# The norm of queries and keys in an encoder layer: eps from a 65th column, the mean's factor in the square's scale

## The chip, the cores and the metric

The kernel runs on one core of a Trainium2 chip. The metric is the device time of one execution in microseconds (us). A core has five engines with an instruction queue each, which run side by side and wait for each other through semaphores: PE (matrix products; its weight loads are listed as PEld), DVE (vector operations), ACT (activations and scaled copies), POOL (a slower general engine) and SP, which here issues the transfers (DMA). An engine takes its own instructions strictly in the order written, so one that waits holds up all behind it.

## The reference

The kernel computes one layer of a hybrid encoder for two sequences with shared weights, 512 tokens (P, "prompt") and 1024 tokens (S, "sample"), 1024 wide, in float32. Cut to what matters here:

```
h = rmsnorm(x, norm_g); proj = h @ w_in
qa, ka, va, za, qb, kb, vb, zb, ga, gb = split(proj)
qa = rmsnorm(qa.reshape(B, L, 8, 64), qn_a);  ka = rmsnorm(ka.reshape(B, L, 8, 64), kn_a)
oa = neighbourhood_attention(qa, ka, va, rpb_a) * silu(za) @ w_o_a      # branch A: 8 heads
qb = rmsnorm(qb.reshape(B, L, 8, 64), qn_b);  kb = rmsnorm(kb.reshape(B, L, 2, 64), kn_b)
ob = window_gqa_attention(qb, kb, vb, t5_table, sink_b) * silu(zb) @ w_o_b   # branch B: 8 query, 2 key heads
y = x + (sigmoid(ga) * oa + sigmoid(gb) * ob) @ w_out

rmsnorm(x, g) = x * rsqrt(mean(x * x) + 1e-6) * g      # over the 64 channels of a head
```

## The kernel before

**Precision.** Every large product is made of three: each operand is split into a rounded part and a rest (hi and lo), and hi·hi, lo·hi and hi·lo are summed in PSUM. ACT writes the rounded part (a copy with a change of type), DVE or POOL subtracts it for the rest (L1172 and L1177 in the dense part, L605 and L610 for the attention weights).

**Stages.** First P's attention, then P's dense part, then S's attention, then S's dense part; the orders overlap where data allow. Attention goes by six groups of heads: four of branch A (two query and two key heads each), two of branch B (four query heads and one key head). For each group and each tile of 128 tokens `project` makes one projection of 384 columns: 24 matmuls (L764) into a PSUM bank p. P has 6 x 4 = 24 such projections and S 6 x 8 = 48, 72 in all, 48 of branch A and 24 of branch B.

**The norm, once per projection.** From the bank p: ACT squares the 4 or 5 heads' columns into sq (L783), DVE sums 64 columns for each head (`tensor_reduce`, L788), POOL multiplies by 1/64 and adds eps (`tensor_scalar`, L795), POOL raises to the power -0.5 (L802), and DVE multiplies q and k by that factor into qk (L819; for branch B the key half by L669 on DVE or L665 on ACT). Beside it ACT and DVE take the values v out of the bank (L809, L812). Then PE transposes qk (L864), ACT and DVE write the transposed parts (L885 to L904), and the scores (L937, L972), the softmax (L981, L1005, and a scaling on POOL L1011 or DVE L1013), the transposes of its result (L1029) and the product with v (L1066) follow. The tile sq has one buffer, so a Square waits for the reduce before it.

**The order.** A planner (`Flow`) records each operation with its engine or engines, a cost in ns, a priority and what it depends on; `run` then plays the operations through a clock of its own, gives each to a free engine by priority, and writes the instructions of every engine in that order. Costs count: an operation that the planner believes to end sooner lets others stand elsewhere, on any engine. Costs of ACT, DVE and POOL in the attention are taken times 1.1 (SLACK), and a hop between engines has its own cost (LAG; 96 ns from POOL to POOL). Operations that DVE or POOL can do go to the one that the planner thinks done first.

Of the kernel before, what the change touches and what calls it, by code (L numbers as in the profile page):

```python
# [40 lines left out]
P = 128  # L41
# [3 lines left out]
EPS = 1e-6  # L45
# [309 lines left out]
def encoder_kernel(  # L355
# [23 lines left out]
    nc = tc.nc  # L379
    act = nc.scalar  # L380
    dve = nc.vector
# [35 lines left out]
    mhalf = cpool.tile([P, 8], F32, tag="mhalf", name="mhalf")  # L417
# [10 lines left out]
    DVE_ = lambda n: 68 + 1.043 * n  # L428
# [3 lines left out]
    f = Flow(pspool)  # L432

    def bank(tag):
        return f.value(pspool, [P, 512], F32, tag, BANKS[tag])
# [215 lines left out]
    def attention_phase(geo, hh, hl, h_ops, mask_d, early, late):  # L651
# [6 lines left out]
        def tile_(shape, dt, tag, bufs):  # L658
            return f.value(early if tag in ("sq", "ss", "rs_v", "rs_r", "v", "q", "qt", "qk") else late, shape, dt, tag, bufs)
# [3 lines left out]
        def copy(e, out, in_, scale=None):  # L663
# [4 lines left out]
            else:  # L668
                engines[e].tensor_scalar(out, in_, scale, None, op0=ALU.mult)  # L669

        a_tables = geo.tables()
        at = np.cumsum([0, *(n for n, _ in a_tables)]).tolist()
        mask = tile_([P, at[-1]], F32, "mask", 1)
# [57 lines left out]
        def project(br, w, t, prio):  # L731

            nq, nk = (2, 2) if br == "A" else (4, 1)
            nn = nq + nk
            ps = bank("p")
# [22 lines left out]
            for k in range(KC):  # L758
                hi, lo = w[k // 2]
                c = slice((k % 2) * GW, (k % 2) * GW + GW)  # L760
                for m, (u, mv) in enumerate(((0, hi), (0, lo), (1, hi))):
# [19 lines left out]
            f.op(  # L781
                (("act", ACT_(nn * 64, False)),),
                lambda e: act.activation(sq.t[:, : nn * 64], ps.t[:, : nn * 64], AF.Square),  # L783
                prio, new=[sq], use=[ps],
            )
            f.op(
                (("dve", DVE_(nn * 64)),),
                lambda e: dve.tensor_reduce(  # L788
                    ss.t[:, :nn], sq.t[:, : nn * 64].rearrange("p (h d) -> p h d", d=64), axis=AX.X, op=ALU.add
                ),  # L790
                prio, new=[ss], use=[sq],
            )
            f.op(
                (("pool", 165),),
                lambda e: nc.gpsimd.tensor_scalar(  # L795
                    rv.t[:, :nn], ss.t[:, :nn], 1.0 / 64, EPS, op0=ALU.mult, op1=ALU.add
                ),
                prio, new=[rv], use=[ss],
            )
            f.op(  # L800
                (("pool", 1000),),
                lambda e: nc.gpsimd.tensor_tensor(r.t[:, :nn], rv.t[:, :nn], mhalf[:, :nn], op=ALU.pow),  # L802
                prio, new=[r], use=[rv],
            )
            nv = GW - nn * 64

# [6 lines left out]
                prio, use=[ps, v], into=[v],  # L813
# [9 lines left out]
                    op=ALU.mult,  # L823
                ),
                prio, new=[qk], use=[ps, r],
# [285 lines left out]
        for gi, (br, g) in enumerate(groups):  # L1111
# [14 lines left out]
            for t in range(nb):  # L1126
                prio = lead + t
# [673 lines left out]
    for i in range(2):  # L1801
        ps, made = bank("x"), []
        for j in range(2):
# [3 lines left out]
                lambda e, ps=ps, cols=cols, out=out: pe.matmul(ps.t[:, out], one, gb.t[:1, cols], start=True, stop=True),  # L1807
# [3 lines left out]
    for t in range(gp.nb):  # L1811
# [4 lines left out]
        for i, (ps, users) in enumerate(gains_row if t == 0 else ()):  # L1816
            gains_row[i][1] = [f.op(
                (("act", ACT_(512, False)),),
                lambda e, ps=ps, i=i: act.activation(gb.t[:, i * 512 : i * 512 + 512], ps.t, AF.Copy),
                NORM[1] - 1, use=[ps], hold=[gb], after=users[2:],  # L1820
            )]
    setup(norm_p, -0.7, h_ops["p"][1][:1])
    expand_ops(gp, [max(-1, (h // 2 - 1) * gp.nb) for h in range(8)], [h_ops["p"][t][:1] for t in (1, 3, 3, 3)])
    o_p, exps, start = attention_phase(gp, *h_p, h_ops["p"], mask_p, early["p"], late["p"])
    rb = f.value(rb_pool, [P, NT_S], F32, "rb", 1)
    r_s = f.value(norm_p, [P, gs.nb], F32, "r_s", 1)
    for t in range(gs.nb):
# [10 lines left out]
        after=[o, f.begun[NT_P, 23]],  # L1838
# [111 lines left out]
```

## Time and profile before

| what | before |
|---|---|
| time, median of 3 runs | 1136.74 us (1136.4 to 1139.61) |
| the profiled execution | 1139.25 us, its span 1137.5 us |
| TensorE clock granted, mean | 0.998 |
| DVE, ACT, POOL busy | 856.8, 651.4, 339.3 us |
| idle time of POOL before the scaling L795, ended by the reduce L788 | 134.0 us in 41 waits |
| power L802, shortest and median | 1006 and 1060 ns |

The span goes from the first to the last instruction of the profiled execution. A row of a group names the line, the engine, the operation, what it writes and reads, the shape and the count; then the busy time of the group in us and the mean of one instruction in ns; then the idle time of its engine just before, and what ended it. A row of the timeline has the start in us, the duration in us, the instruction, and in brackets the idle time before it and what ended that.

### The profile page before, as it was taken

The page shows a single profiled execution, that of the slowest core. Times are in us where ns is not written, and L with a number is a line of the kernel's source. Part 1 is how long each engine was busy: PE and PEld are TensorE (multiplying, and loading weights), DVE is VectorE, ACT ScalarE, POOL GpSimd, SP SyncE. Part 2 cuts the span into 40 slices and gives each one's busy share as a digit, 9 for nine tenths or more (in the row PEclk, how much of TensorE's full clock was granted, in tenths as well). Part 3 has the DMA queues.
Part 4 walks back from the last instruction along what each step waited for, and adds up shares of the span by engine and source line. Part 5 has one row for each costly group of instructions (what it writes and reads, how often), then busy time and mean ns, then how long its engine had stood idle before and what let it go on. Part 6 is the DMA issues. An engine that isn't in the chain of part 4 may idle for free.

```text
span 1137.5 us, 18703 instructions
## 1 busy us (share of the span) xinstructions
PE 1121.8 (99%) x6079; PEld 975.1 (86%) x6079; DVE 856.8 (75%) x1988; ACT 651.4 (57%) x1499; POOL 339.3 (30%) x438
## 2 busy tenths in 40 slices
PE   8999999999999999999999999999999999999998
PEld 6999988888888889999999988988788888888877
DVE  5878797587776568787878889876988766767564
ACT  5777987644532247565769888877543435333430
POOL 3654433000011144434324343510333323123111
PEclk9999999999999999999999999999999999999999
DMA  7854543488785743121213214244888645756862
GB/s 257 273 159 138 185 115 103 107 254 257 246 286 202 249 138 91 29 61 29 82 41 93 73 38 119 50 131 138 288 261 237 206 158 191 278 197 224 262 208 93
DMA packets 139108, 186.11 MB, mean 164 GB/s; under 512 B 29897, under 2 KB 68561, under 8 KB 139010
## 3 DMA queue, kind: packets, MB, share of 16 engines
q1 hardware_dynamic: 139010, 184.91, 51.8%
q8 instruction: 48, 0.79, 0.3%
q14 instruction: 50, 0.41, 0.1%
HBM read 137.66 MB, written 51.92 MB: 167 GB/s over the span
## 4 chain that ended last, share of the span: by engine, by line
PE 90%; DMA 4%; DVE 2%; ACT 1%; issue 1%; SPq 1%; POOL 0%; ACTq 0%; DVEq 0%
PE p L764 26%; PE x L1293 8%; PE x L1295 8%; PE x L1294 8%; PE x L1066 5%; PE x L1029 5%; PE x L937 5%; PE p L1294 4%; PE p L1295 4%; PE p L1293 4%; PE d L1293 4%; PE d L1295 4%; PE d L1294 4%; PE x L864 2%; DMA w<-in_w_att_dram 1%; DMA U<-m_d 1%
## 5 line engine op out<-in xcount | busy, mean ns | idle before, releaser
L764 PE MATMUL p<-whi,hh 128*128 128x384 f32 x384 | 133.7, 348 | 0.0
L764 PE MATMUL p<-whi,hl 128*128 128x384 f32 x384 | 132.6, 345 | 0.0
L764 PE MATMUL p<-wlo,hh 128*128 128x384 f32 x384 | 132.0, 344 | 0.0
L1172 ACT ACTIVATE whi<-raw 128x512 fp32r<-128x512 f32 (+1 forms) x140 | 81.5, 600 | 73.0 <-PE x L1294 22.5
L981 ACT ACTIVATE sb<-sb,mx 128x384 f32<-128x384 f32 (+1 forms) x192 | 107.7, 565 | 16.9 <-DVE mx L972 16.6
L1294 PE MATMUL x<-T,whi 128*128 128x512 f32 x280 | 108.9, 389 | 0.0
L1293 PE MATMUL x<-T,whi 128*128 128x512 f32 x280 | 108.9, 389 | 0.0
L1295 PE MATMUL x<-T,wlo 128*128 128x512 f32 x280 | 108.9, 389 | 0.0
L764 PE MATMUL p<-whi,hb 128*128 128x384 f32 x384 | 107.6, 346 | 0.0
L1177 DVE TENSOR_TENSOR wlo<-raw,whi 128x512 fp32r<-128x512 f32 (+1 forms) x110 | 73.4, 678 | 34.5 <-ACT whi L1172 31.0
L1177 POOL TENSOR_TENSOR wlo<-raw,whi 128x512 fp32r<-128x512 f32 (+1 forms) x30 | 36.4, 1219 | 210.2 <-ACT whi L1172 210.2
L1040 DVE TENSOR_TENSOR pp<-x,pp 128x512 fp32r<-128x512 f32 (+1 forms) x136 | 82.6, 639 | 19.2 <-ACT pp L1035 18.5
L802 POOL TENSOR_TENSOR rs_r<-rs_v,mhalf 128x4 f32<-128x4 f32 (+1 forms) x72 | 80.7, 1121 | 5.7
L1293 PE MATMUL x<-hh,whi 128*128 128x512 f32 x200 | 78.4, 392 | 2.1 <-ACT fh L1440 2.1
L1035 ACT ACTIVATE pp<-x 128x512 fp32r<-128x512 f32 (+1 forms) x136 | 70.9, 561 | 15.2 <-PE x L1029 14.0
L1295 PE MATMUL x<-hh,wlo 128*128 128x512 f32 x200 | 78.5, 393 | 0.0
L1294 PE MATMUL x<-hl,whi 128*128 128x512 f32 x200 | 78.3, 392 | 0.0
L1066 PE MATMUL x<-pp,v 128*128 128x256 f32 (+1 forms) x368 | 75.8, 322 | 0.0
L764 PEld LDWEIGHTS p<-whi,hl 128*128 128x128 f32 x384 | 72.8, 190 | 1.3 <-issue 1.0
L764 PEld LDWEIGHTS p<-wlo,hh 128*128 128x128 f32 x384 | 73.0, 190 | 1.0 <-issue 0.7
L764 PEld LDWEIGHTS p<-whi,hh 128*128 128x128 f32 x384 | 73.0, 190 | 0.7 <-DVE v L812 0.3
L764 PEld LDWEIGHTS p<-whi,hb 128*128 128x128 f32 x384 | 69.1, 188 | 3.0 <-issue 1.3
(388 smaller groups left out, 2967.8 us busy)
## 6 DMA issues: line engine op xcount, KB each, us to landing
raw<-in_w_g_dram SPq DMA_DIRECT2D x84, 256.0 KB
w<-in_w_att_dram SPq DMA_DIRECT2D x46, 384.0 KB
raw<-in_w_z_dram SPq DMA_DIRECT2D x40, 256.0 KB
ot<-o_d SPq DMA_DIRECT2D x36, 256.0 KB
g_d<-C SPq DMA_DIRECT2D x34, 256.0 KB
fr<-in_w_g_dram SPq DMA_DIRECT2D x28, 256.0 KB
raw<-in_w_out_dram SPq DMA_DIRECT2D x28, 256.0 KB
out_dram<-C SPq DMA_DIRECT2D x19, 256.0 KB
```

Source lines behind the costliest of these rows:

```text
L764: pe.matmul(ps.t[:, :GW], part[u](k), mv.t[:, c], start=k == 0 and m == 0, stop=k == KC - 1 and m == 2,)
L802: lambda e: nc.gpsimd.tensor_tensor(r.t[:, :nn], rv.t[:, :nn], mhalf[:, :nn], op=ALU.pow),
L937: pe.matmul(pss[2 * pair + i].t[:, :width], q.t[rows, u, at : at + P], kv[:, tiles[0] : tiles[-1] + 1 : step], start=n == 0, stop=n == 2,)
L981: act.activation(sb.t[:, :width], sb.t[:, :width], AF.Exp, bias=mx.t[:, i : i + 1], scale=-1.0, accum_out=sm.t[:, i : i + 1],)
L1035: lambda e, pt=pt, pp=pp, nn=nn: act.activation(pp.t[:, 0, :nn], pt.t[:, :nn], AF.Copy),
L1040: lambda e, pt=pt, pp=pp, nn=nn: dve.tensor_tensor(pp.t[:, 1, :nn], pt.t[:, :nn], pp.t[:, 0, :nn].bitcast(F32), op=ALU.subtract),
L1066: pe.matmul(out(), v.t[:, vs], mv(), start=first, stop=last)
L1172: (("act", ACT_(n)),), lambda e: act.activation(hi(), src(), AF.Copy), prio,
L1177: lambda e: engines[e].tensor_tensor(lo(), src(), hi().bitcast(F32), op=ALU.subtract), prio,
L1293: pe.matmul(out, hi.t[:, cs], mh(), start=first and k == 0, stop=False, **more)
L1294: pe.matmul(out, hi.t[:, cs], ml(), start=False, stop=False, **more)
L1295: pe.matmul(out, lo.t[:, cs], mh(), start=False, stop=last and k == len(ws) - 1, **more)
```

## The change

The tile sq is made once for a whole attention phase and has 65 columns for each of five heads. A memset on POOL at the head of the phase writes eps into each 65th column. Square is given the scale 0.125, so that it writes (x/8)^2 = x^2/64, into the first 64 columns of each head; the reduce sums 65 columns, and so gives mean plus eps. The scaling on POOL (L795) and its tile rs_v are gone, and the power reads the reduce's result. Square waits for the reduce before it, as before.

```diff
@@ -668,6 +668,9 @@
+        sq = tile_([P, 336], F32, "sq", 1)
+        sqv = lambda n: sq.t[:, : n * 65].rearrange("p (h d) -> p h d", d=65)
+        sq_ops = [f.op((("pool", 100),), lambda e: nc.gpsimd.memset(sqv(5)[:, :, 64:], EPS), -0.5, new=[sq])]
         a_tables = geo.tables()
...
@@ -773,34 +776,25 @@
-            sq = tile_([P, 320], F32, "sq", 1)
             ss = tile_([P, 8], F32, "ss", 2)
-            rv = tile_([P, 8], F32, "rs_v", 2)
             r = tile_([P, 8], F32, "rs_r", 2)
             v = tile_([P, 256], F32R, "v", 7 if nt == NT_S else 6)
             f.op(
                 (("act", ACT_(nn * 64, False)),),
-                lambda e: act.activation(sq.t[:, : nn * 64], ps.t[:, : nn * 64], AF.Square),
-                prio, new=[sq], use=[ps],
-            )
-            f.op(
-                (("dve", DVE_(nn * 64)),),
-                lambda e: dve.tensor_reduce(
-                    ss.t[:, :nn], sq.t[:, : nn * 64].rearrange("p (h d) -> p h d", d=64), axis=AX.X, op=ALU.add
+                lambda e: act.activation(
+                    sqv(nn)[:, :, :64], ps.t[:, : nn * 64].rearrange("p (h d) -> p h d", d=64), AF.Square, scale=0.125
                 ),
-                prio, new=[ss], use=[sq],
-            )
-            f.op(
-                (("pool", 165),),
-                lambda e: nc.gpsimd.tensor_scalar(
-                    rv.t[:, :nn], ss.t[:, :nn], 1.0 / 64, EPS, op0=ALU.mult, op1=ALU.add
-                ),
-                prio, new=[rv], use=[ss],
-            )
+                prio, use=[ps], hold=[sq], after=sq_ops[-1:],
+            )
+            sq_ops.append(f.op(
+                (("dve", DVE_(nn * 65)),),
+                lambda e: dve.tensor_reduce(ss.t[:, :nn], sqv(nn), axis=AX.X, op=ALU.add),
+                prio, new=[ss], hold=[sq], after=f.ops[-1:],
+            ))
             f.op(
                 (("pool", 1000),),
-                lambda e: nc.gpsimd.tensor_tensor(r.t[:, :nn], rv.t[:, :nn], mhalf[:, :nn], op=ALU.pow),
-                prio, new=[r], use=[rv],
+                lambda e: nc.gpsimd.tensor_tensor(r.t[:, :nn], ss.t[:, :nn], mhalf[:, :nn], op=ALU.pow),
+                prio, new=[r], use=[ss],
             )
```

The planner now writes another order on every engine. In the changed file lines stand elsewhere: the reduce is L791 (before L788), the power L796 (L802), v L806 (L812), qk L813 (L819), qk's transposes L858 (L864), the projection's matmuls L767 (L764), the scores L966 (L972), the reciprocal L999 (L1005), sums L1160 (L1166), subtractions L1171 (L1177), the tables L701 (L698).

At the start of S's attention, POOL before (raw<-raw are sums of weights, fl the rest of a weight in the dense part, rs_r the power's result):

```order
L1166 TENSOR_TENSOR raw<-raw 128x512 x4
L1177 TENSOR_TENSOR fl<-fr,fh 128x512
L795 TENSOR_SCALAR rs_v<-ss 128x4
L802 TENSOR_TENSOR rs_r<-rs_v,mhalf 128x4
L795 TENSOR_SCALAR rs_v<-ss 128x4
L802 TENSOR_TENSOR rs_r<-rs_v,mhalf 128x4
L698 TENSOR_TENSOR bias<-mask,raw 128x16x8
```

and now:

```order
L1160 TENSOR_TENSOR raw<-raw 128x512
L673 MEMSET sq 128x5
L1160 TENSOR_TENSOR raw<-raw 128x512 x3
L1171 TENSOR_TENSOR fl<-fr,fh 128x512
L796 TENSOR_TENSOR rs_r<-ss,mhalf 128x4 x2
L701 TENSOR_TENSOR bias<-mask,raw 128x16x8
```

The second memset stands among the four sums, and the power comes straight after fl. On PE, at the same place, 24 matmuls of the second projection are followed by three product steps of three matmuls before (L1293 to L1295, into the bank d) and by two now, and then by the transposes of qk.

In P's attention, where the second projection's qk is made, DVE before (xt is a tile of x that is being normed, hl the rest of its transposed norm, bias a table):

```order
L523 SCALAR_TENSOR_TENSOR xt<-xt,nr,rb 128x512
L698 TENSOR_TENSOR bias<-mask,raw 128x32x4
L698 TENSOR_TENSOR bias<-mask,raw 128x16x4 x3
L698 TENSOR_TENSOR bias<-mask,raw 128x32x4 x2
L698 TENSOR_TENSOR bias<-mask,raw 128x16x4 x4
L523 SCALAR_TENSOR_TENSOR xt<-xt,nr,rb 128x512
L545 TENSOR_TENSOR hl<-x,hh 128x4x128
L812 TENSOR_TENSOR v<-p,v 128x2x64
L819 TENSOR_TENSOR qk<-p,rs_r 128x256
```

and now:

```order
L806 TENSOR_TENSOR v<-p,v 128x2x64
L545 TENSOR_TENSOR hl<-x,hh 128x4x128
L701 TENSOR_TENSOR bias<-mask,raw 128x32x4
L701 TENSOR_TENSOR bias<-mask,raw 128x16x4 x4
L701 TENSOR_TENSOR bias<-mask,raw 128x32x4
L701 TENSOR_TENSOR bias<-mask,raw 128x16x4 x4
L523 SCALAR_TENSOR_TENSOR xt<-xt,nr,rb 128x512 x2
L813 TENSOR_TENSOR qk<-p,rs_r 128x256
```

The second subtraction for hl and that for v no longer stand between L523 and qk.

In P's branch B, the 20th projection, DVE before, from its reduce on:

```order
L788 TENSOR_REDUCE ss<-sq 128x5
L1616 COPY fc<-d 128x512
L667 CAST hb<-hl 128x512
L1177 TENSOR_TENSOR fl<-fr,fh 128x512
L1005 RECIPROCAL rs<-sm 128x4
L972 ISA sb,mx<-x,bias,nsink 128x384
L972 ISA mx 128x1
L812 TENSOR_TENSOR v<-p,v 128x64
```

and now:

```order
L791 TENSOR_REDUCE ss<-sq 128x5
L806 TENSOR_TENSOR v<-p,v 128x64
L667 CAST hb<-hl 128x512
L1171 TENSOR_TENSOR fl<-fr,fh 128x512
L813 TENSOR_TENSOR qk<-p,rs_r 128x256
L999 RECIPROCAL rs<-sm 128x4
L669 TENSOR_SCALAR qk<-p,rs_r 128x128
```

Before, three more scores follow those rows, then qk (L819), a cast to hb and the key half (L669). So a copy and four scores stood ahead of qk, and now none does. On PE 56 instructions stood between that projection's last matmul and the transposes of its qk; now 30 do.

More of the change, by code (lines that the diff above doesn't have):

```diff
@@ L782, in project @@
                 (("act", ACT_(nn * 64, False)),),
-                lambda e: act.activation(sq.t[:, : nn * 64], ps.t[:, : nn * 64], AF.Square),
-                prio, new=[sq], use=[ps],
-            )
-            f.op(
-                (("dve", DVE_(nn * 64)),),
-                lambda e: dve.tensor_reduce(
-                    ss.t[:, :nn], sq.t[:, : nn * 64].rearrange("p (h d) -> p h d", d=64), axis=AX.X, op=ALU.add
-                ),
-                prio, new=[ss], use=[sq],
-            )
-            f.op(
-                (("pool", 165),),
-                lambda e: nc.gpsimd.tensor_scalar(
-                    rv.t[:, :nn], ss.t[:, :nn], 1.0 / 64, EPS, op0=ALU.mult, op1=ALU.add
-                ),
-                prio, new=[rv], use=[ss],
-            )
+                lambda e: act.activation(
+                    sqv(nn)[:, :, :64], ps.t[:, : nn * 64].rearrange("p (h d) -> p h d", d=64), AF.Square, scale=0.125
+                ),
+                prio, use=[ps], hold=[sq], after=sq_ops[-1:],
+            )
+            sq_ops.append(f.op(
[3 more added lines that the diff above has]
+            ))
             f.op(
                 (("pool", 1000),),
-                lambda e: nc.gpsimd.tensor_tensor(r.t[:, :nn], rv.t[:, :nn], mhalf[:, :nn], op=ALU.pow),
-                prio, new=[r], use=[rv],
+                lambda e: nc.gpsimd.tensor_tensor(r.t[:, :nn], ss.t[:, :nn], mhalf[:, :nn], op=ALU.pow),
+                prio, new=[r], use=[ss],
             )
```

## The prediction

> **What bounds the kernel now.** I read the page's busy times first, then who waited for whom on PE, then the groups of the norm's instructions, and last the timeline at each place where PE stood still. The first row of the page, and the waits of PE (waiter, released by, then us in total, times, the longest):
>
> ```profile
> PE 1121.8 (99%) x6079; PEld 975.1 (86%) x6079; DVE 856.8 (75%) x1988; ACT 651.4 (57%) x1499; POOL 339.3 (30%) x438
> ...
> PE x L1807 <- DMA rb<-in_norm_row_dram: 4.6, 1, 4.6
> PE x L864 <- DVE qk L819: 2.4, 2, 1.9
> PE x L1293 <- ACT fh L1440: 2.1, 1, 2.1
> PE d L1294 <- DVE T L1177: 1.3, 1, 1.3
> PE x L535 <- DVE xt L523: 1.0, 1, 1.0
> PE p L1293 <- ACT whi L1172: 0.5, 1, 0.5
> ```
>
> PE is the bound, and hardly ever waits: 1137.5 - 1121.8 = 15.7 us of the span are free, and these six rows are 11.9 of them. Only the second row belongs to what is changed: 2.4 us, in two places, in which the transposes of qk (L864) wait for the multiplication by the norm's factor (L819). That is 0.2% of the time. The other 70 norms are hidden: PE works on later projections, scores or dense products until qk is there. So shortening the norm can win 2.4 us at most by itself; whatever else happens comes from the planner, which orders all engines anew when one cost changes.
>
> **The change part by part.** The groups of the norm before, by shape (count, then busy us and mean ns of one, then idle before):
>
> ```profile
> L802 POOL TENSOR_TENSOR rs_r<-rs_v,mhalf 128x4 f32<-128x4 f32 x48 | 51.0, 1064 | 3.7
> L795 POOL TENSOR_SCALAR rs_v<-ss 128x4 f32<-128x4 f32 x48 | 15.3, 318 | 101.0 <-DVE ss L788 99.5
> ...
> L783 ACT ACTIVATE sq<-p 128x256 f32<-128x256 f32 x48 | 18.4, 383 | 15.2 <-PE p L764 12.3 <-DVE qk L819 1.3 <-ACT q L899 0.5
> L809 ACT ACTIVATE v<-p 128x128 fp32r<-128x128 f32 x48 | 13.3, 277 | 0.0
> L783 ACT ACTIVATE sq<-p 128x320 f32<-128x320 f32 x24 | 10.4, 435 | 1.1 <-PE p L764 1.0
> ...
> L788 DVE TENSOR_REDUCE ss<-sq 128x4 f32<-128x256 f32 x48 | 19.7, 411 | 5.1 <-ACT sq L783 4.9
> ```
>
> *Removed:* 72 scalings on POOL (L795), 318 ns each in the mean over the 48 of branch A: some 23 us of POOL's 339.3, and as much from the chain Square, reduce, scaling, power, multiplication. POOL is 30% busy, so its time as such is worth nothing; the chain is covered by PE's other work in all but the two places.
>
> *Square:* it now writes 64 columns, leaves one, and so on, and its scale is no longer one. The row of L809 writes with gaps too. From 256 to 320 columns Square grows by 435 - 383 = 52 ns, 0.81 ns a column, so 128 columns without gaps would take 279; L809 takes 277. A gap costs nothing: 0. *Reduce:* 4 or 5 columns more on 256 or 320; if all of its 411 ns went with the columns, 4 x 1.6 = 6.4 ns each, 0.5 us on DVE in 72, hidden since DVE has a quarter of the span free: 0, and at most 0.5 bare.
>
> *Two memsets added on POOL.* The timeline of POOL, with idle time before in brackets:
>
> ```profile
> 0.24 0.10 POOL L1929 MEMSET const-float32-0.0<- 128x1 f32 x1 [0.24 <-issue]
> ...
> 5.53 0.19 POOL L467 TENSOR_SCALAR nv<-ns 128x1 f32<-128x1 f32 x1 [4.24 <-ACT junk L463]
> ...
> 390.83 1.80 POOL L1166 TENSOR_TENSOR raw<-raw 128x512 f32<-128x512 f32 x1 [13.29 <-DVE raw L1166]
> ```
>
> A small memset is 0.10 us. The first stands ahead of 4.24 us in which POOL idles, the second among the four sums of L1166, before the last of which POOL idles 13.29 us. Both 0; bare, 0.10 each. Behind them are queued the identity's second half and the next sum, which have that same idle time.
>
> *The place at 406 us,* where the second sequence's attention starts. POOL, DVE, PE:
>
> ```profile
> 404.49 1.31 POOL L1177 TENSOR_TENSOR fl<-fr,fh 128x512 fp32r<-128x512 f32 x1 [11.86 <-ACT fh L1172]
> 405.88 1.17 POOL L795 TENSOR_SCALAR rs_v<-ss 128x4 f32<-128x4 f32 x1
> 407.13 1.01 POOL L802 TENSOR_TENSOR rs_r<-rs_v,mhalf 128x4 f32<-128x4 f32 x1
> 408.23 0.19 POOL L795 TENSOR_SCALAR rs_v<-ss 128x4 f32<-128x4 f32 x1
> ...
> 404.89 2.10 DVE L667 CAST hb<-hl 128x512 fp32r<-128x512 f32 x2
> 408.18 0.42 DVE L819 TENSOR_TENSOR qk<-p,rs_r 128x256 f32<-128x256 f32 x1 [0.69 <-POOL rs_r L802]
> ...
> 405.18 0.39 PE L1293 MATMUL d<-hh,fh 128*128 128x512 f32 x1
> 405.87 0.39 PE L1293 MATMUL d<-hh,fh 128*128 128x512 f32 x1
> 408.66 0.44 PE L864 MATMUL x<-ident,qk 128*128 128x128 f32 x2 [1.94 <-DVE qk L819]
> ```
>
> Here the scaling took 1.17 us where the next one took 0.19, and ended as DVE's two casts did (404.89 + 2.10 = 406.99). With it gone the power starts at 405.88. Either it is held by the casts as the scaling was, ends at about 407.05 + 1.01 = 408.06 instead of 408.14, and saves 0.08; or it runs at once, ends at 406.89, and qk follows the casts at 407.0, 1.18 earlier. The nearest row is the scaling itself, an instruction of the same engine at the same moment: 0.08. Against that, the planner counts on the shorter chain: PE's order has two product steps of three matmuls ahead of L864 where it had three, one step of 405.87 - 405.18 = 0.69 us put behind it. PE arrives 0.69 earlier and waits for the same chain: 0.69 - 0.08 = **+0.6 us**, with bounds 0.69 - 1.18 = -0.5 and +0.6. The Trainium skill, "SBUF — State Buffer", § Who interferes with whom, has a rule that speaks against this part of the change: a cast on VectorE in its two-port mode takes the port pair that it shares with GpSimd for a whole instruction, and the other engine blocks until the end. The 1.17 beside 0.19 agrees; by that rule it would be the +0.6, without it the -0.5.
>
> *The place at 30 us.* DVE, and PE behind it:
>
> ```profile
> 28.60 0.82 DVE L523 SCALAR_TENSOR_TENSOR xt<-xt,nr,rb 128x512 f32<-128x512 f32 x1
> 29.34 0.68 DVE L545 TENSOR_TENSOR hl<-x,hh 128x512 fp32r<-128x512 f32 x1
> 29.94 0.27 DVE L812 TENSOR_TENSOR v<-p,v 128x128 fp32r<-128x128 f32 x1
> 30.14 0.41 DVE L819 TENSOR_TENSOR qk<-p,rs_r 128x256 f32<-128x256 f32 x1
> ...
> 30.69 0.41 PE L864 MATMUL x<-ident,qk 128*128 128x128 f32 x2 [0.48 <-DVE qk L819]
> ```
>
> The factor was long there; qk stood behind L545 and L812 on DVE. In the new order both are out of its way (one later, one earlier), so it can start up to 30.14 - 29.34 = 0.8 us sooner, and the wait of 0.48 goes: **-0.5**, bounds -0.5 and 0.
>
> *Everything the planner moves beside that.* PE's rows at the end of the part that is reordered and behind it:
>
> ```profile
> 813.95 0.50 PE L1294 MATMUL d<-T,whi 128*128 128x512 f32 x1 [1.30 <-DVE T L1177]
> ...
> 821.22 0.39 PE L1293 MATMUL x<-T,whi 128*128 128x512 f32 x1
> ...
> 1085.98 0.50 PE L1293 MATMUL x<-hh,whi 128*128 128x512 f32 x1 [2.09 <-ACT fh L1440]
> ```
>
> PE has the same instructions, and its last 1375 of 6076, from the row at 821.22 on, stand in the same order, with the wait of 2.1 for L1440 among them; so do the 831 that end just before the place at 406 us, with the wait of 0.5 for L1172. Neither goes. The wait of 1.3 for T lies where the order is new: gone or doubled, -1.3 to +1.3; I take 0, since nothing in the change touches T or its subtraction.
>
> Sum: 0.6 - 0.5 = **+0.1 us** on the profiled execution's 1139.25 (span 1137.5 and 1.75 around it), and the same on the median of the runs, 1136.74, which is 2.5 below it: **1136.8**. From the bounds alone: -0.5 - 0.5 - 1.3 = -2.3, and 0.6 + 0.2 + 0.5 + 1.3 = +2.6.
>
> **The rivals.** (1) *Faster:* the time that POOL and the chain gain empties the waits. All of those that lie where the order is new would go: 2.4 and 1.3, so 1136.7 - 3.7 = **1133.0**. For it: PE waits nowhere else. Against it: half of this is the place at 406 us, where the casts hold POOL whatever it runs. Beyond this there is nothing to win, since PE's own work is the same.
>
> (2) *Slower:* the new order moves L864 forward on PE further than the chain gets shorter. Its place is branch B, where DVE has the longest queues. At 147 us:
>
> ```profile
> 147.42 0.47 DVE L788 TENSOR_REDUCE ss<-sq 128x5 f32<-128x320 f32 x1
> 152.45 0.41 DVE L819 TENSOR_TENSOR qk<-p,rs_r 128x256 f32<-128x256 f32 x1
> 153.33 0.34 DVE L669 TENSOR_SCALAR qk<-p,rs_r 128x128 f32<-128x128 f32 x1
> ...
> 152.75 0.34 PE L764 MATMUL p<-wlo,hb 128*128 128x384 f32 x1
> 152.92 1.04 PE L1029 MATMUL x<-ident,sb 128*128 128x128 f32 x8
> 153.71 0.59 PE L764 MATMUL p<-whi,hb 128*128 128x384 f32 x2
> 154.32 0.49 PE L864 MATMUL x<-ident,qk 128*128 128x128 f32 x3
> ```
>
> Between the projection's last matmul and L864 PE has 56 instructions before and 30 now; 14 of L764 (152.92 - 152.75 = 0.17 apart), the eight of L1029 (0.79 until the next) and one product step of 0.69 are gone, 3.9 us of cover. There was 154.32 - 153.67 = 0.65 to spare. If qk and its key half came as late after the reduce as before, less the scaling's 0.32, PE would stand 3.9 - 0.65 - 0.3 = 2.9 us. The order says otherwise: four scores, a copy and an idle moment are no longer ahead of qk on DVE, nor a cast ahead of the key half. But that is the planner's reckoning, and other places in branch B lose cover too (78 instructions to 32 at one in the second sequence). It decides from a little over one such place; two make 1136.8 + 5.8 = **1142.6**.
>
> (3) *The change doesn't do what it says:* a gap in Square's output, or a power that takes over the scaling's waits, leaves the chain as long as it was. Then only the +0.69 and the -0.5 remain: 1136.9, inside the forecast.
>
> **How the numbers follow.** A measurement of this kernel tells about 0.3%, 3.4 us, from no change. The forecast with (3) has 0.66, (1) 0.13, (2) 0.21. (1) just reaches 0.3%, so faster by more is 0.12, and the rest of it goes to no change; (2) is slower. No change: 0.67. The bounds of the terms give 1134.5 to 1139.3 for the likeliest case alone; to leave out no more than 2 in 10, I go down to (1) and up most of the way to (2): 1133.0 to 1141.5.
>
> **What would show it.** Right: PE busy within 1 us of 1121.8; no L795; Square and reduce within 10 ns of their rows; the wait of L864 at the start of the second sequence's attention at 1.9 to 2.7 us and that at 30 us gone; POOL's power there ending with or after DVE's casts. Wrong: waits of PE for L819 or L669 in branch B that add up to over 3 us, or a sum of PE's waits under 9 us.

## The result, and the profile after

| | before | after |
|---|---|---|
| time, median of 6 runs | 1138.17 us (1136.40 to 1139.92) | 1146.82 us (1142.51 to 1150.65) |
| the profiled execution, its span | 1139.25, 1137.5 us | 1145.95, 1144.2 us |
| sum of PE's idle time, PE busy | 15.7, 1121.8 us | 20.6, 1123.6 us |

The ratio of the runs is 1.0071 with a 95% interval of [1.0045, 1.0097]. The change makes the kernel 0.7% slower. The forecast was no change, 1136.8 us in a range of 1133.0 to 1141.5; the kernel is slower than all of that range.

The first row of after's page, the busy times:

```profile
PE 1123.6 (98%) x6079; PEld 975.1 (85%) x6079; DVE 857.9 (75%) x1971; ACT 652.1 (57%) x1502; POOL 322.7 (28%) x382
```

And the waits of PE (waiter, released by, then us in total, times, the longest):

```profile
PE x L1801 <- DMA rb<-in_norm_row_dram: 4.6, 1, 4.6
PE x L858 <- DVE qk L813: 3.3, 5, 1.4
PE x L1287 <- ACT hh L1166: 3.1, 1, 3.1
PE x L1060 <- DVE pp L1034: 1.4, 1, 1.4
PE x L535 <- DVE xt L523: 1.1, 1, 1.1
PE x L1023 <- DVE sb L1007: 1.1, 2, 0.9
PE d L1287 <- ACT fc L1610: 1.1, 2, 0.7
PE x L1287 <- ACT fh L1434: 1.0, 1, 1.0
```

The third of these rows is new, and it is the longest single wait that before doesn't have. Nothing in it belongs to the norm: PE waits for hh, the rounded part of a gated row in P's dense part. PE's timeline there:

```profile
358.28 0.40 PE L1289 MATMUL x<-hh,wlo 128*128 128x512 f32 x1
361.79 0.50 PE L1287 MATMUL x<-hh,whi 128*128 128x512 f32 x1 [3.12 <-ACT hh L1166]
...
363.54 0.63 PE L1288 MATMUL x<-hl,whi 128*128 128x512 f32 x1
363.96 0.63 PE L1289 MATMUL x<-hh,wlo 128*128 128x512 f32 x1
...
367.20 0.39 PE L1289 MATMUL x<-hh,wlo 128*128 128x512 f32 x1
367.43 0.40 PE L1287 MATMUL x<-hh,whi 128*128 128x512 f32 x1
```

Two things are to be seen. PE stands still for 3.12 us. And for some 3.5 us after it the same matmul starts every 0.42 to 0.43 us and lasts 0.63; by 367 us it is back to 0.23 and 0.39. The busy time by stretch has that as a granted clock (the number after the busy times, ahead of the share of the DMA engines) under 1:

```profile
340.00:350.00 10.00, 10.00 (x46) 8.28 (x45) 7.33 (x12) 4.92 (x9) 1.30 (x1) 1.00 0.75 234
...
360.00:365.00 5.00, 2.98 (x8) 2.19 (x9) 3.02 (x5) 1.26 (x2) 0.00 (x0) 0.81 0.77 251
365.00:370.00 5.00, 5.00 (x21) 4.03 (x20) 1.94 (x3) 1.90 (x3) 0.00 (x0) 0.85 0.64 175
370.00:380.00 10.00, 10.00 (x46) 8.29 (x45) 4.17 (x7) 0.79 (x2) 1.28 (x1) 1.00 0.88 293
```

5 x (1 - 0.81) + 5 x (1 - 0.85) = 1.7 us are lost behind the wait. Matched matmul by matmul, PE in after is 2.0 us later than before from 219 to 357 us, and 7.8 at 378. So 5.8 of the 6.7 us by which the two profiled executions differ arise here, in a stretch in which PE's order did not change. The rest nearly cancels: +2.0 in P's attention, -1.1 between this place and S's attention, +2.7 in S's attention, and -2.7 at 1086 us, where the profile of before has its wait of 2.09 us with a lower clock behind it.

Why hh was late is read from ACT and PE. Before, hh was written at 354.24 + 0.63 = 354.87, and PE read it at 356.26 without a wait, 1.39 us later:

```profile
354.24 0.63 ACT L1172 ACTIVATE hh<-C 128x512 fp32r<-128x512 f32 x1 [4.57 <-DVE C L1166]
...
356.26 0.39 PE L1293 MATMUL x<-hh,whi 128*128 128x512 f32 x1
```

After, the same row of ACT stands 6.87 us later, while PE would have come 2.0 later:

```profile
361.11 0.63 ACT L1166 ACTIVATE hh<-C 128x512 fp32r<-128x512 f32 x1 [4.54 <-DVE C L1160]
```

6.87 - 2.02 - 1.39 = 3.46, which is the delay to 0.05 us (of which 3.12 is idle time). The lateness builds up in a chain beside PE (load of x, norm, store, gate, hh): in P's dense part DVE also norms S's x, two tiles at a time, from x loaded by SP (L558) into two buffers, and DVE and SP take the gates, the weights' rests (wlo) and those loads in turn. SP's last pair of x loads starts at 297.61 us in the timeline of before:

```profile
297.61 1.78 SPq L558 DMA_DIRECT2D xt<-in_xt_s_dram  x2
```

and at 302.58 in that of after:

```profile
302.58 1.84 SPq L558 DMA_DIRECT2D xt<-in_xt_s_dram  x2
```

That is 5.0 us late, of which PE's own lateness explains 2.0. In this stretch the order of SP, DVE and ACT did change, although PE's did not.

### The profile page after: what moved, and what is told of

It reads as the page before. It is cut to its first block, busy times and chain, and to the rows that moved or that the text cites. A ratio compares the mean times of both kernels' runs of the same rounds, so it can differ in the third digit from the quotient of the medians.

```text
span 1144.2 us, 18686 instructions
## 1 busy us (share of the span) xinstructions
PE 1123.6 (98%) x6079; PEld 975.1 (85%) x6079; DVE 857.9 (75%) x1971; ACT 652.1 (57%) x1502; POOL 322.7 (28%) x382
## 4 chain that ended last, share of the span: by engine, by line
PE 75%; DMA 9%; DVE 6%; issue 4%; ACT 3%; POOL 2%; SPq 1%; POOLq 0%; ACTq 0%; DVEq 0%
PE p L767 21%; PE x L1287 6%; PE x L1288 6%; PE x L1289 6%; PE x L1060 5%; PE x L1023 4%; PE x L931 4%; PE d L1287 3%; PE d L1289 3%; PE d L1288 3%; PE p L1287 3%; PE p L1289 3%; PE p L1288 3%; DMA w<-in_w_att_dram 2%; PE x L858 2%
## 5 line engine op out<-in xcount | busy, mean ns | idle before, releaser
L767 PE MATMUL p<-whi,hh 128*128 128x384 f32 x384 | 133.7, 349 | 0.0
L767 PE MATMUL p<-wlo,hh 128*128 128x384 f32 x384 | 131.9, 344 | 0.0
L767 PE MATMUL p<-whi,hl 128*128 128x384 f32 x384 | 131.9, 344 | 0.1
L796 POOL TENSOR_TENSOR rs_r<-ss,mhalf 128x4 f32<-128x4 f32 (+1 forms) x72 | 89.4, 1242 | 140.6 <-DVE ss L791 136.1
L1166 ACT ACTIVATE whi<-raw 128x512 fp32r<-128x512 f32 (+1 forms) x140 | 81.7, 600 | 76.0 <-PE x L1288 24.4
L767 PE MATMUL p<-whi,hb 128*128 128x384 f32 x384 | 107.0, 346 | 0.0
L1171 DVE TENSOR_TENSOR wlo<-raw,whi 128x512 fp32r<-128x512 f32 (+1 forms) x111 | 74.8, 683 | 32.4 <-ACT whi L1166 26.6
L1171 POOL TENSOR_TENSOR wlo<-raw,whi 128x512 fp32r<-128x512 f32 (+1 forms) x29 | 35.3, 1223 | 211.1 <-ACT whi L1166 211.0
L767 PEld LDWEIGHTS p<-whi,hl 128*128 128x128 f32 x384 | 72.8, 190 | 1.5 <-issue 1.0
L767 PEld LDWEIGHTS p<-whi,hh 128*128 128x128 f32 x384 | 72.8, 190 | 0.7 <-issue 0.5
L767 PEld LDWEIGHTS p<-wlo,hh 128*128 128x128 f32 x384 | 72.9, 190 | 0.5 <-issue 0.5
L767 PEld LDWEIGHTS p<-whi,hb 128*128 128x128 f32 x384 | 69.4, 188 | 3.2 <-issue 0.8
```

Source lines behind the costliest of these rows:

```text
L767: pe.matmul(ps.t[:, :GW], part[u](k), mv.t[:, c], start=k == 0 and m == 0, stop=k == KC - 1 and m == 2,)
L796: lambda e: nc.gpsimd.tensor_tensor(r.t[:, :nn], ss.t[:, :nn], mhalf[:, :nn], op=ALU.pow),
L1166: (("act", ACT_(n)),), lambda e: act.activation(hi(), src(), AF.Copy), prio,
L1171: lambda e: engines[e].tensor_tensor(lo(), src(), hi().bitcast(F32), op=ALU.subtract), prio,
```

## The experiments

Theory: the new order costs the time, above all what it does to that chain in P's dense part; the new instructions cost nothing. Main rival: the instructions (gaps, 65 columns, the power that waits for a port). Times of before are of the same chip and job, 1136.7 to 1137.8 us.

### New instructions in the old order, old instructions in the new order

The planner is told of operations that emit nothing, or an operation emits two instructions, so that order and instructions come apart:

```diff
 (("pool", 165),),
-lambda e: nc.gpsimd.tensor_scalar(rv.t[:, :nn], ss.t[:, :nn], 1.0 / 64, EPS, ...),
+lambda e: None,          # the planner still counts it; Square, reduce and power are the changed ones
```

> The changed kernel's instructions (Square with scale 0.125 into 65-column heads, reduce of 65 columns, eps by a memset, no scaling) in the order of the kernel before: the planner still sees the scaling as an operation of 165 ns, which emits nothing. The order of PE, SP, DVE and ACT is that of before instruction by instruction; POOL lacks the scalings and has two memsets. Theory 'order' (the planner's new order lost the 8 us): no difference from before, 1136 to 1140 us, and no PE wait over 1.5 us near 360 us. Rival 'instructions' (gaps in Square's output, a longer reduce or a power that now waits for the port cost it): as the changed kernel, about 1147 us.

Measured: 1140.89 us (1135.50 to 1146.76), 1.0036 [1.0015, 1.0057]. Between the two expectations: 3.7 us over before, without a wait over 0.2 us near 360 us.

```diff
 (("pool", 1000),),
+# emits: rv <- ss / 64 + eps, then the power of rv; Square and reduce as before
```

> The instructions of the kernel before (Square without gaps, reduce of 64 columns, scaling and power on POOL) in the changed kernel's order: the planner plans as in the changed kernel, and the power's operation emits scaling and power. Theory 'order': as slow as the changed kernel, 1144 to 1150 us, with a PE wait of about 3 us near 362 us; the 72 scalings may add up to 1 us. Rival 'instructions': as before, 1136 to 1140 us.

Measured: 1145.95 us (1140.75 to 1149.73), 1.0075 [1.0054, 1.0097]: as slow as the changed kernel with the instructions of before. PE's waits of 340 to 380 us have the long one:

```profile
PE x L1291 <- ACT hh L1170: 2.9, 1, 2.9
```

So the new order alone is enough for the whole loss. That the new instructions also cost something in the old order was not expected, and is taken up below.

### Which phase's order

```diff
+old = nt in (NT_P,)      # in the other kernel (NT_S,): this phase is planned with the scaling
```

> The changed kernel, but P's attention is planned as before (the planner sees the scaling there, and it emits nothing); S's attention is planned as in the changed kernel. By the two traces PE loses 2.0 us by 219 us and 5.8 more at 355 to 378 us, and in S -1.1 at its start, +2.4 by 479 us and -2.7 at 1083 us. Theory 'order in P' (P's new order makes the side work of P's dense part late): the 7.8 us are gone, and 1138.2 - 1.3 = 1137 us remain. Rival 'order in S': 1146 us.

> The other half: P's attention is planned as in the changed kernel, S's attention as before. Theory 'order in P': 1138.2 + 7.8 = 1146 us, with the PE wait of about 3 us near 362 us. Rival 'order in S': 1138 us.

Measured: with the old order in P 1141.02 us, 1.0045 [1.0024, 1.0066]; with the old order in S 1145.60 us, 1.0080 [1.0057, 1.0102], with the wait in P's dense part at its old length:

```profile
PE x L1306 <- ACT hh L1185: 3.1, 1, 3.1
```

P's new order with S's old one costs 8.4 us, as expected (some of it may be the moved tiles that this kernel has in S, below). The wait for hh is 2.9 to 3.1 us in the three profiles with P's new order (the changed kernel, the old instructions in the new order, and the old order in S), and at most 0.8 in the eight that have P's old order and load nothing twice. The kernel with the old order in P doesn't come down to 1137 us. Its profile has 4.2 us of waits for qk in three places of S, one of them 1.91 us long and followed by a lower clock, so the new order of S may cost something. The runs don't show that: the first experiment's kernel, with the old order in S too, takes 1140.9 us, as long as this one, for reasons that lie in P's opening and in the place of the tiles (below). So the 3.9 us are not divided here, and the two losses (8.4 and 3.9) can't be added.

### The chain in P's dense part, relieved and lengthened

```diff
+kd = 2 if t % 4 > 1 else KC           # two blocks of eight are loaded and used
-xt.t.rearrange("p (k n) -> p k n", n=P), x_t[:, :, tok]...
+xt.t.rearrange("p (k n) -> p k n", n=P)[:, :kd], x_t[:kd, :, tok]...
```

> The changed kernel, in the same order, but the four loads of x for S's norm in the last two rounds of P's dense part fetch 2 of 8 blocks, and the norm uses those two blocks in place of all eight (so S's numbers are not the reference's; all operations stay, of four loads three quarters of the bytes are gone). Theory 'late side chain' (in P's dense part PE waits 3.1 us at 362 us for hh, because the chain load of x, norm, store, gate, hh is late by 4 to 7 us from 260 us on; that wait and the lower clock after it cost 5 to 6 us): the wait is under 1 us, no lower clock there, and 1140 to 1143 us. Rival (hh is late for another reason, such as the weights' subtractions on DVE): still 1145 to 1148 us.

Measured: 1141.42 us, 1.0043 [1.0027, 1.0059]. The wait is gone (0.2 us for hl is left), and the busy time by stretch has a clock of 1.00 there:

```profile
360.00:380.00 20.00, 20.00 (x89) 16.55 (x90) 9.67 (x15) 5.05 (x8) 1.43 (x2) 1.00 0.71 225
```

The order of every engine is that of the changed kernel. Over the before of its own job the loss is 4.1 us by medians, where the changed kernel lost 8.7 (1.0043 against 1.0071 by ratio, 3.2 us). Matched matmul by matmul, its profile gains 5.0 us on that of the changed kernel at this place and loses 0.6 in all the rest. So the wait and what follows it cost 3 to 5 us, and they come from the chain through the loads of x. Which link of the chain is late isn't told apart, as shorter loads also leave the transfers behind them more room. The other side:

```diff
-nc.sync.dma_start(xt.t..., x_t[:, :, tok]...)
+[nc.sync.dma_start(xt.t..., x_t[:, :, tok]...) for _ in range(2 if t == 7 else 1)]
```

> The kernel before, with one transfer more: in the last round of P's dense part the load of x for S's seventh tile is made twice, one behind the other, which makes that side chain some 5 us later. Theory 'late side chain' (before, it had about 2 us to spare): a PE wait of 2 to 3.5 us for hh near 355 us and a lower clock behind it, 1137.2 + 5 = 1142 us (1140.5 to 1144). Rival (the chain has room): no wait, 1137 us.

Measured: 1140.51 us, 1.0021 [1.0004, 1.0038]. One transfer more, and the kernel before has the wait:

```profile
PE x L1295 <- ACT hh L1174: 1.8, 1, 1.8
```

and the lower clock, in the busy time by stretch:

```profile
340.00:360.00 20.00, 17.96 (x73) 14.24 (x72) 14.04 (x22) 6.53 (x12) 2.98 (x2) 0.92 0.61 187
```

In the profiled execution the place costs 4.1 us (PE 1.84 us ahead of before at 353 us, 2.22 behind at 380). Not all of that is the transfer's: in the fourteenth run's profile (below), which loads nothing twice and has PE 1.87 us ahead, the place costs 1.2, and PE waits 0.4 us for hh. The difference, 2.9, agrees with the runs, 2 to 3 us, less than the 5 expected. The chain had little room before, as the 1.39 us say.

### What a wait of PE costs beside itself

```diff
+zero()                                # small matmul with a zero operand
+for _ in range(r):
+    act.activation(dump, ident, AF.Copy, scale=0.0)
+zero()                                # waits for the r writes on ACT
```

> The kernel before, with six artificial waits of PE in S's dense part, some 34 us apart: a small matmul with a zero operand waits for 3, 5, 8, 11, 15 and 20 writes of that operand on ACT, which wait for a matmul before; by the writes that is about 1.1, 1.5, 2.1, 2.7, 3.5 and 4.5 us, 15 us together. Theory 'clock' (a wait of PE of up to 1.6 us costs only itself, one of 1.9 us or more also lowers the granted clock behind it and costs about 2 us more): the last four are followed by a stretch with a granted clock under 0.95, and the time is 1137 + 15 + 8 = 1160 us. Rival (a wait costs itself alone): 1152 us.

Measured: 1174.97 us, 1.0331 [1.0310, 1.0352]. The writes on ACT came 0.34 us apart, not 0.2, and ACT began some of them late (2.4 us after the small matmul in the second wait), so the waits were 1.08, 3.97, 4.99, 3.81, 5.17 and 7.99 us, and the expected time is missed by their length. What each cost in all, from the start of the next matmuls against before, less 0.46 us for the two small matmuls themselves, was 1.06, 5.56, 7.14, 6.20, 7.02 and 9.91: nothing beside itself for the first, and 1.6, 2.2, 2.4, 1.9 and 1.9 for the others. The third wait in the busy time by stretch:

```profile
850.00:880.00 30.00, 30.00 (x134) 24.86 (x133) 24.22 (x35) 12.74 (x25) 11.28 (x10) 1.00 0.78 226
880.00:890.00 10.00, 5.01 (x15) 3.87 (x14) 4.61 (x8) 3.83 (x11) 0.10 (x1) 0.66 0.57 188
890.00:920.00 30.00, 30.00 (x133) 24.77 (x133) 17.94 (x30) 10.27 (x21) 8.25 (x8) 1.00 0.44 144
```

and PE's timeline behind it:

```profile
885.57 0.42 PE L1301 MATMUL x<-T,dump 128*128 128x64 f32 x1 [4.99 <-ACT dump L1304]
...
887.65 0.63 PE L1307 MATMUL x<-T,wlo 128*128 128x512 f32 x1
```

So a wait of 3.8 to 8.0 us costs about 2 us more, and no more for the longest than for the shortest. The rival (itself alone) is out: the waits add up to 27.0, the loss is 37.7.

### What the new instructions cost in the old order

The first experiment's profile shows a second effect: PE's drift against before grows evenly through the attention, with no wait in it. The groups of PE in S's attention, before (count, busy us, mean ns):

```profile
L764 PE MATMUL p<-whi,hb 128*128 128x384 f32 x250 | 70.4, 347 | 0.0
L764 PE MATMUL p<-whi,hl 128*128 128x384 f32 x149 | 51.5, 345 | 0.0
...
L764 PE MATMUL p<-wlo,hb 128*128 128x384 f32 x125 | 43.0, 344 | 0.0
```

and with the instructions and the order of before, but tiles at other addresses (the ninth run, below):

```profile
L766 PE MATMUL p<-whi,hb 128*128 128x384 f32 x250 | 71.1, 349 | 0.0
L766 PE MATMUL p<-whi,hl 128*128 128x384 f32 x148 | 51.3, 347 | 0.0
...
L766 PE MATMUL p<-wlo,hb 128*128 128x384 f32 x125 | 43.3, 346 | 0.0
```

The kernels that tell it apart: the first experiment with the scaling in the first four projections; that one's tiles with the instructions of before; the first experiment with tiles of the old size; and both together.

```diff
-lambda e: None,
+lambda e: nc.gpsimd.tensor_scalar(rv.t[:, :nn], mean.t[:, :nn], 1.0, 0.0, ...) if nt == NT_P and prio < nb else None,
```

> The first experiment's kernel (the changed instructions in the order of before, 1140.9 us), but POOL runs the scaling, with factor 1, in the first four projections of P; the other 68 are left out. Theory 'opening' (without the scaling POOL starts its subtraction for wlo, L610, earlier, a 0.22 us table operation of DVE then waits for it, and PE stands 2.75 us for xt at 30 us and runs at a lower clock after): as before, 1136 to 1138.5 us, and that wait is under 1.1 us. Rival 'the instructions themselves' (Square, reduce or the other 68 powers): still about 1141 us.

Measured: 1139.84 us, 1.0022 [1.0009, 1.0035]. PE waits no longer for xt at 30 us, but 2.5 us remain, between the two expectations.

```diff
-sq = tile_([P, 320], F32, "sq", 1)
+sq = tile_([P, 1], F32, "sq", 1)      # counted by the planner; Square writes into sq65 of 336 columns
+mean = f.value(early, [P, 8], F32, "mean", 4)
```

> The kernel before, instruction by instruction and in its order, with only the tiles of the fifth experiment: Square writes into a tile of 336 columns that is made once, the reduce into a tile of four buffers of its own, and the tile that the planner counts is one column, so tiles of the attention stand at other addresses. In the fifth and the first experiment PE's projection matmuls that read hb and hl, and the scores, take about 2 ns more each than before (347 to 349, 345 to 346, 352 to 354 in the row of S's attention), 2.6 us in all. Theory 'place of the tiles': 1137.3 + 2.5 = 1140 us, and the same 2 ns. Rival 'the new instructions' (their traffic beside PE): 1136 to 1138.5 us and the durations of before.

Measured: 1139.10 us, 1.0012 [0.9990, 1.0033]: in time not to be told from before, but the 2 ns are there, in the rows above, with not one changed instruction. So they belong to the place of the tiles. They come again in other profiles: the mean of whi,hb from 420 to 810 us is 346.7 to 346.9 ns in all five with the tiles of before or their size (before and the seventh, eighth, thirteenth and fourteenth runs), and 348.8 to 349.1 in the four with the moved ones (first, fourth, fifth, ninth).

```diff
-mean = f.value(early, [P, 8], F32, "mean", 4)
+mean = f.value(early, [P, 8], F32, "mean", 2)
+for planned in (sq, ss, rv):
+    planned.make = lambda: None       # takes no memory
```

> The first experiment again (the changed instructions in the order of before), with tiles of the same total size as before: sq of 336 columns and the reduce's tile of two buffers take the 1408 bytes that sq, ss and rs_v took; what the planner counts takes no memory. Theory 'place of the tiles and opening': the matmuls take 347, 345 and 344 ns again as before, and the time is 1137.5 to 1139.5 us, what is over 1137.5 being runs in which PE waits for xt at 30 us. Rival 'the instructions': 1140 us or more, as in the first experiment.

Measured: 1140.81 us, 1.0037 [1.0016, 1.0058]. The matmuls are at 347 and 345 ns again and the even drift is gone, but the time isn't lower: the opening costs it. The timeline of POOL and DVE there:

```profile
25.07 1.50 POOL L815 TENSOR_TENSOR rs_r<-mean,mhalf 128x4 f32<-128x4 f32 x1
...
26.85 1.83 POOL L610 TENSOR_TENSOR wlo<-w,whi 128x768 fp32r<-128x768 f32 x1
...
25.61 4.51 DVE L700 TENSOR_TENSOR bias<-mask,raw 128x128 f32<-128x128 f32 x10
```

With four scalings put back, in place:

```diff
-lambda e: None,
+lambda e: nc.gpsimd.tensor_scalar(mean.t[:, :nn], mean.t[:, :nn], 1.0, 0.0, ...) if nt == NT_P and prio < nb else None,
```

> The kernel with the changed instructions in the old order and tiles of the old size, but POOL runs the scaling, with factor 1 and in place, in the first four projections of P. Theory 'opening and place of the tiles are all': as before, a ratio of 0.998 to 1.002, no PE wait over 1.1 us for xt at 30 us, and the matmuls at 347, 345 and 344 ns. Rival 'something else in the changed instructions': a ratio over 1.002, as the thirteenth run's 1.0037.

Measured: 1137.45 us, 0.9995 [0.9983, 1.0007]: not to be told from before. The same rows of its timeline:

```profile
24.72 0.69 POOL L810 TENSOR_SCALAR mean<-mean 128x4 f32<-128x4 f32 x1
25.49 1.08 POOL L817 TENSOR_TENSOR rs_r<-mean,mhalf 128x4 f32<-128x4 f32 x1
...
27.06 2.27 POOL L610 TENSOR_TENSOR wlo<-w,whi 128x768 fp32r<-128x768 f32 x1
...
25.27 1.64 DVE L700 TENSOR_TENSOR bias<-mask,raw 128x128 f32<-128x128 f32 x10
```

The ten table operations take 1.64 us with the scaling and 4.51 without. Without it POOL's wlo starts at 26.85, ahead of the last tables; with it at 27.06, when the ten have ended (25.27 + 1.64 = 26.91) and DVE's next operation has begun. In the first case DVE stands for POOL, and PE for xt (2.8 us, then a lower clock). The Trainium skill, "SBUF — State Buffer", § Who interferes with whom, says that the engine which issues first keeps the shared pair for a whole instruction and the other blocks, also for a two-input operation of VectorE against a reading one of GpSimd. The traces agree: the ten take 4.51 - 1.64 = 2.9 us longer, about the length of wlo (1.83) and of the subtraction that POOL has right behind it (1.27); it falls on two of the ten, of 1.87 and 1.30 us, where the others of that shape take 0.21.

So of the instructions themselves nothing is left that the runs can tell: 68 scalings fewer, 4 or 5 columns more, gaps in Square's output, all together 0.9995. The fifth run has the four scalings too, though not in place, and the moved tiles: its 1.0022 [1.0009, 1.0035] is clear of this one's, and so the place of the tiles shows in time.

### Other costs for the power

```diff
-(("pool", 1000),)
+(("pool", 1261),)        # in the other kernels 1130 and 900
```

> The changed kernel, but the planner takes 1261 ns for the power instead of 1000, so that it counts on a chain as long as before (165 + 96 + 1000). All instructions are the changed kernel's; only the order is another. Theory 'order' (what the change costs is decided by where the new order puts P's side work against the transfers): without a wait over 1.7 us near 360 us it takes 1136 to 1141 us, with one 1143 to 1148. Rival 'the shorter chain' (a planner that counts on the shorter chain is what helps or harms): as before, 1137 us, since the count is that of before.

> The same with 1130 ns for the power, which with the planner's factor of 1.1 is the 1242 ns that it took in the changed kernel. Theory 'order': another time again, 1135 to 1148 us, as its waits fall; nothing makes it better than the planner's wrong 1000. Rival 'true costs': a planner that knows the true cost orders better, at most 1138 us.

> The same with 900 ns, further from the truth. Theory 'order': a time between 1135 and 1148 us like the others, not in the order of the costs. Rival 'true costs': slower than the changed kernel, over 1147 us.

Measured: 1142.83 us, 1.0048 [1.0028, 1.0069]; 1144.79, 1.0058 [1.0037, 1.0078]; 1150.83, 1.0110 [1.0071, 1.0148]. The instructions are those of the changed kernel in all three. 1261 is over the expected 1141: its wait for hh is 1.1 us, but two others, for xt (1.66) and for whi, were followed by a lower clock. 900 is over the 1148 expected, and over 1147, as its rival said. Knowing the true cost did not bring back the old time (1130: 1144.79), nor did counting on the old chain (1261, 5.3 us over before). With 1000 the four orders give 1142.8 to 1150.8, and none is as fast as before: the old order is the odd one. The expectation that the times would not go in the order of the costs failed: the ratios are 1.0110, 1.0071, 1.0058 and 1.0048 for 900, 1000, 1130 and 1261. Four orders can fall so by chance, so it is open whether a longer planned cost as such makes a better order here. No version that beats before came out of this.

## Why the prediction was wrong, step by step

**What bounds the kernel.** PE is the bound, as said. The profile's waits of PE were read and their margins were not: the row of hh with 1.39 us to spare never was.

**The norm's own instructions.** Right. Square takes 382 and 443 ns where it took 383 and 435, and the reduce of 260 columns 415 where 256 took 411:

```profile
L784 ACT ACTIVATE sq<-p 128x256 f32<-128x256 f32 x48 | 18.4, 382 | 15.0 <-PE p L767 14.5 <-ACT q L893 0.3
L784 ACT ACTIVATE sq<-p 128x320 f32<-128x320 f32 x24 | 10.6, 443 | 2.3 <-PE p L767 2.2
...
L791 DVE TENSOR_REDUCE ss<-sq 128x4 f32<-128x260 f32 x48 | 19.9, 415 | 8.8 <-ACT sq L784 8.3
...
L796 POOL TENSOR_TENSOR rs_r<-ss,mhalf 128x4 f32<-128x4 f32 x48 | 56.1, 1169 | 102.4 <-DVE ss L791 102.3
```

The power took over part of the scaling's waits, 1169 ns in place of 1064, as rival (3) allowed, at no price in most places (0.2 us at 30 us, below). "The scaling is hidden" holds for the time of POOL, with one exception that only the old order has: in the opening, four scalings kept POOL from being early.

**The place at 406 us** (+0.6, wait 1.9 to 2.7). Half right. PE does come 0.68 us earlier behind its projection, with two product steps in place of three, and the power is held by the casts (1.51 us for 1.01 alone) and ends behind them. DVE's reduce before and after, the casts, the power and what follows:

```profile
404.36 0.41 DVE L788 TENSOR_REDUCE ss<-sq 128x4 f32<-128x256 f32 x1
...
410.68 0.41 DVE L791 TENSOR_REDUCE ss<-sq 128x4 f32<-128x260 f32 x1
...
411.21 2.02 DVE L667 CAST hb<-hl 128x512 fp32r<-128x512 f32 x2
412.07 1.51 POOL L796 TENSOR_TENSOR rs_r<-ss,mhalf 128x4 f32<-128x4 f32 x1
413.61 0.42 DVE L813 TENSOR_TENSOR qk<-p,rs_r 128x256 f32<-128x256 f32 x1 [0.38 <-POOL rs_r L796]
...
414.09 0.44 PE L858 MATMUL x<-ident,qk 128*128 128x128 f32 x2 [1.39 <-DVE qk L813]
```

But the casts did not hold all of it: the power ends at 413.58, 0.35 us behind the casts (413.23), where the scaling and power of before ended 1.15 behind theirs (408.14 against 406.99). From the start of the reduce to that of qk it is 3.82 us before (404.36 to 408.18) and 2.93 after, 0.89 less, where the term had 0.08. The reduce itself also came 0.34 earlier against PE. 0.68 - 0.89 - 0.34 = -0.55: PE waits 1.39 us in place of 1.94, and of the two bounds the term took the wrong one. One execution is not enough to size such a term, though. In the eight profiles with the old order in both phases PE waits 0.0 to 2.1 us at this very instruction.

**The place at 30 us** (-0.5). Wrong: 0.71 us, more than the 0.48 of before. The step took for granted that "the factor was long there". In the new order the power ran beside the ten table operations on DVE:

```profile
26.02 3.86 POOL L796 TENSOR_TENSOR rs_r<-ss,mhalf 128x4 f32<-128x4 f32 x1
```

**"Everything the planner moves beside that"** is the step that failed. It held that where PE's order stays, PE's waits stay: "Neither goes". (The profile has 6079 instructions of PE, not 6076; nothing hangs on that.) But a new wait of 3.1 us came inside the 831 instructions that were in the same order; the wait of 0.5 for L1172 went, that of 1.3 for T went too, and L1440's went from 2.1 to 1.0. The order of PE says what PE asks for; when it is there is decided by SP, DVE and ACT, whose order and start did change. Nor are the waits of one profile those of the kernel: in the seven other profiles with the old order in both phases, L1440's wait is 0.0 to 1.0 us, so the 2.1 belonged to the execution that the prediction was made from, and the one for L1172 is 0.0 to 1.6. The step also counted a wait at its length. Behind the 2.09 us of before the clock had dropped as well, which a row of before would have shown:

```profile
1080.00:1100.00 20.00, 17.91 (x73) 14.30 (x72) 12.95 (x22) 8.15 (x16) 3.12 (x4) 0.91 0.61 202
```

20 x 0.09 = 1.8 us, nearly as much again as the 2.09 that PE stood still. The sum was made from the waits that were to be seen, so a wait that arises elsewhere had no term, and the bounds (-2.3 to +2.6) held none.

**The rivals.** (2) had the right sign, and with 1142.6 the nearer time, for the wrong reason: no wait of PE over 0.1 us for L813 or L669 lies in either branch B of the profiled execution, so the cover of qk's transposes was enough there. (1) did not come. The true rival, an order that makes a chain of transfers late in a place that was not reordered on PE, was not among them.

**What would show it.** Of the signs for right, no L795, the durations and the power behind the casts came; PE busy (1.8 us more; not by the clock, since either profile has one such stretch of half rate), the wait at 406 us and that at 30 us did not. Of the signs for wrong neither came: no waits in branch B, and a sum of PE's waits over 9. That the sum could rise was not on the list.

**What stays open.** The short loads leave 1141.4 us, 4 over before. Its profile has waits of 1.1 us for sb, 1.4 for pp and 1.0 for qk that before doesn't have, but none of them was tried by itself. Why the order of before beats the others is not shown, nor why the new order has the loads of x late.

## What to carry to other kernels

Where a planner orders all engines anew, cost a small edit by the margins, not by the waits: look in the trace of before for the operands that are ready only a microsecond or two ahead of the engine that bounds, and ask of each whether the queues behind it moved. A comparison of the bounding engine's order alone tells nothing about that. Read the waits from more than one profile of before: here one place had 0.0 to 2.1 us with the same order. To learn whether an edit or its order moved the time, run the new instructions in the old order and the old ones in the new.

## What the runs showed of the hardware that was not expected

- A wait of PE has a second price. Over all profiles here, none of the 21 waits between 1.2 and 1.64 us was followed by a lower clock; of nine between 1.66 and 1.94 us five were; so were all thirteen of 2.09 us and over inside the program. Where the lower clock came, the trace's record of it has half rate for 3.41 us or twice that, some of it still in the wait, and PE lost 1.6 to 3.4 us by it; the loss did not grow with the wait (3.1 and 3.4 behind waits of 2.75 and 2.10 us, 2.1 behind one of 7.99). At the program's start PE is slow as well: in the profile of before its matmuls of 384 columns start 0.32 us apart up to 15.2 us and 0.17 to 0.18 apart after that. The views show 1.00 there because the record begins only at 15.4 us. The Trainium skill, "TensorE: Matmul & The Clock Gate", Part 1, describes a clock halved after an idle window of about 3.4 us, in windows that run free. The half rate for one or two such lengths (0.43 us in place of 0.23 a matmul) and the chance near the limit agree; that the whole window must be idle does not, since waits of 1.66 and 1.78 us were enough.
- Moving tiles in memory by some two hundred bytes (by their sizes), with the same instructions in the same order, made PE's 384-column matmuls that read hb and hl some 2 ns slower (345 to 347, 347 to 349), and those that read hh less than 1 ns. With the old size of the tiles they were back. Why is not shown.
